# Hybrid decoder trunk on one core: the opening's squares, condition row and first loads moved to other engines and queues

## The chip, the cores and the metric

The kernel runs on 1 core of one Trainium2 chip. The metric is the device time in microseconds. The core has five engines that run side by side and wait for one another by semaphores: TensorE (PE, with its weight loads as PEld), VectorE (DVE), ScalarE (ACT), GpSimd (POOL) and SyncE (SP), which here only issues transfers. Transfers (DMAs) can be issued from SP's queue (hardware queue q1) or from POOL's (software queue q0).

## What is computed

The reference is a two-layer decoder trunk in float32, on x of 512 tokens by 1024 channels. Each layer is a half-step SwiGLU FFN, a token mixer and another half-step FFN; the mixer is a short gated convolution in layer 0 and a sparse attention (NSA) in layer 1. Each of the six sub-layers starts with an RMS norm with shift, scale and gate taken from a condition vector c:

```python
cond = jax.nn.silu(c)
mod = (cond @ ada_w[i] + ada_b[i]).reshape(bsz, 3, 3, D_MODEL)
shift, scl, gate = mod[:, :, 0], mod[:, :, 1], mod[:, :, 2]
h = adaln(x, norm_g[i, 0], shift[:, 0], scl[:, 0])
x = x + HALF * gate[:, 0, None, :] * swiglu(h, ffn_w_in[i, 0], ffn_w_out[i, 0])
```

where `adaln` is `rms_norm(x, g) * (1 + scale) + shift`. For the opening it matters that nothing of the first FFN can be multiplied before the norm of x (the mean square over all 1024 channels of each token) and the first scales and shifts (products of the condition vector with rows of `ada_w`) are there.

## The kernel before, in words

**Layout.** x is held transposed, as eight tiles `x[0]` to `x[7]` of 128 channels by 512 tokens. Products are made in three passes for accuracy: each operand is split into a high part (`hi`, made by ACT, line 164) and a remainder (`lo`, made by DVE, line 165), and `mm3` (lines 167 to 170) multiplies hi by hi, hi by lo and lo by hi. The profile's `whi` and `wlo` are those of a weight tile, `hhi` and `hlo` (lines 285, 286) those of the normed x.

**Loads ahead of the work** (lines 89 to 93). SP's queue issues six x tiles and then `cond`, which is c read 128 times from DRAM so that each partition has the whole row; POOL's queue issues the last two x tiles, the norm gains `ngs` and the biases `adabs`. Then POOL makes the identity `ident`. ACT turns cond into its Silu at line 107.

**Modulation** (`ada_tile`, line 115). One tile is 128 rows of the transposed `ada_w`, 512 KB, loaded on SP's queue into a buffer `adaraw`, of which the pool `ada` has four. DVE multiplies it by cond and sums along the row in one instruction (line 119) to 128 values of `mods`. There are 144 such tiles. `ada_scale` and `ada_shift` (lines 123 to 131) add the biases and gains. `ada_first` (line 141) makes the 16 tiles of the first sub-layer's scale and shift, two for each channel block d, in pairs of blocks from d = 2 on. `ada_jobs` makes the others, spread over the following work.

**The first norm** (`Norm.start`, line 261, under high priority). ACT squares each x tile (line 266), DVE adds the squares into `nacc` (line 268), four products with a column of ones sum `nacc` over the partitions into a PSUM tile `pr` (line 270), DVE takes the mean (`nv`, line 272) and the reciprocal root by Newton steps (`rsqrt`, lines 195 to 204), scales the identity by it (`dg`, line 277), and two products with a matrix of ones spread it over all partitions (line 278). `Norm.whole(d)` (line 281) then makes `xr` (DVE, line 284), `hhi` (ACT) and `hlo` (DVE) of block d.

**The first FFN** (`ffn_first`, line 419). Its opening is a loop over the eight blocks d: modulate block d, load and split one of six head weights while d < 6 (`ffn_in`, which calls `weights`; loads at line 179 on SP's queue), norm block d, and multiply it into all head products whose weights are there. The six products accumulate in six PSUM tiles `hs`. After them come the ordinary tiles (`pair`, products named `gu`), whose weights `weights` loads on SP's queue too. The raw weights have three buffers in the pool `wp`, used by the first three head weights, and two in the pool `ada` for the others.

**What sets the order.** Nothing is ordered by hand on the engines: the framework takes the instructions of each engine by the order of the program and by priority, and may put an instruction that it finds ready ahead of one that it finds waiting. A queue of transfers is issued in order, so a load that waits for a buffer holds back those behind it.

Of the kernel before, what the change touches and what calls it, by code (L numbers as in the profile page):

```python
# [12 lines left out]
F32 = mybir.dt.float32  # L13
F32R = mybir.dt.float32r
I32 = mybir.dt.int32
AF = mybir.ActivationFunctionType
ALU = mybir.AluOpType
# [4 lines left out]
P = 128  # L22
D = 1024
T = 512
HT = T // 2
KD = D // P
# [4 lines left out]
NB = T // P  # L31
# [12 lines left out]
NADA = 24  # L44
# [8 lines left out]
def decoder_kernel(ctx, tc, xT, cT, ng, adaw, adab, ffi, ffo, cwi, cw, cwo,  # L53
                   nwi, nwg, pos, w1, w2, qg, kg, nwo, rb, onehot, rowok, out):
    nc = tc.nc
# [15 lines left out]
    def psum(name, tag="mm"):  # L71
        tag = next(six) if tag == "mm" else {"pr": "o"}.get(tag, tag)
        return ps.tile([P, T], F32, name=name, tag=tag, bufs=2)
# [4 lines left out]
    def tmp(name, n=T, tag="t"):  # L78
        bufs, size = TAGS[tag]
        return tp.tile([P, n], F32, name=name, tag=tag, padded_shape=[P, size], bufs=bufs)  # L80


    ada_es = ctx.enter_context(ExitStack())
    ap = ada_es.enter_context(tc.tile_pool(name="ada", bufs=4))
    cond = ap.tile([P, D], F32, name="cond", bufs=1)
    x = [cst.tile([P, T], F32, name=f"x{d}") for d in range(KD)]
    ngs = cst.tile([P, NSUB * KD], F32, name="ngs")
    adabs = cst.tile([P, NSUB * NMOD], F32, name="adabs")
    for d in range(KD):
        (nc.sync if d < KD - 2 else nc.gpsimd).dma_start(x[d], xT[d])  # L90
    nc.sync.dma_start(cond, bass.AP(tensor=cT.tensor, offset=cT.offset, ap=[[0, P], [1, D]]))
    nc.gpsimd.dma_start(ngs, ng)
    nc.gpsimd.dma_start(adabs, adab)
    one = ap.tile([P, 1], F32, name="one", bufs=1)
# [4 lines left out]
    ones = cst.tile([P, P], F32, name="ones")  # L99
# [4 lines left out]
    rowm = cst.tile([P, 1], F32, name="rowm")  # L104
    mods = cst.tile([P, NSUB * NMOD], F32, name="mods")

    nc.scalar.activation(cond, cond, AF.Silu)

    def mod(s, kind, d):
        c = s * NMOD + kind * KD + d  # L110
# [1 line left out]

    def ada_tile(ap, s, t):
        raw = ap.tile([P, D], F32, name="adaraw")
        nc.sync.dma_start(raw, adaw[s * NADA + t])
        m = mods[:, s * NMOD + t:s * NMOD + t + 1]
        nc.vector.tensor_tensor_reduce(out=raw, in0=raw, in1=cond, scale=1.0, scalar=0.0,  # L119
                                       op0=ALU.mult, op1=ALU.add, accum_out=m)  # L120
# [21 lines left out]
    def ada_first(ap, d):  # L142
        n = 1 if d < 2 else 2
        if d % n == 0:
            for c in range(d, d + n):
                ada_tile(ap, 0, c)
                ada_tile(ap, 0, KD + c)
            ada_scale(0, d, d + n)
            ada_shift(0, d, d + n)

# [18 lines left out]
        nc.tensor.matmul(o, sh, ml, start=False, stop=False)  # L169
        nc.tensor.matmul(o, sl, mh, start=False, stop=last)  # L170

    def weights(src, nk, ncol, own=None, held=3, raws=None, to=None):
        def part(name, dt, bufs, from_):
            return (from_ or wp).tile([P, nk * ncol], dt, name=name, tag=name, padded_shape=[P, KD * P], bufs=bufs)

        hi, lo = to or (part("whi", F32R, held, own), part("wlo", F32R, held, own))
        raws = raws or own
        raw = part("wraw", F32, 3 if raws in (None, wp) else 2, raws)
        nc.sync.dma_start(raw.rearrange("p (a n) -> p a n", a=src.shape[1]), src)
        split(raw, hi, lo)  # L180
        return [t.rearrange("p (k n) -> p k n", n=ncol) for t in (hi, lo)]

# [35 lines left out]
    class Norm:  # L218
# [42 lines left out]
        def start(self):  # L261
            pv = self.all = psum("pr", "pr")
            with tc.high_priority():
                for d in range(KD):
                    dst = self.acc if d == 0 else tmp("sq", tag="sq")
                    nc.scalar.activation(dst, x[d], AF.Square)
                    if d:
                        nc.vector.tensor_tensor(self.acc, self.acc, dst, ALU.add)
                for t in range(NB):
                    nc.tensor.matmul(pv[:, t:t + 1], self.acc[:, t * P:(t + 1) * P], ones[:, 0:1], start=True, stop=True)  # L270
                v = sp.tile([P, NB], F32, name="nv", tag="nv", padded_shape=[P, NB])
                nc.vector.tensor_scalar(v, pv[:, 0:NB], 1.0 / D, EPS, op0=ALU.mult, op1=ALU.add)
                r = rsqrt(v, NB)
                dg = tmp("dg").rearrange("p (a b) -> p a b", a=NB)
                for hf in range(2):
                    for t in range(2 * hf, 2 * hf + 2):
                        nc.vector.tensor_scalar(dg[:, t, :], ident, r[:, t:t + 1], None, op0=ALU.mult)
                    nc.tensor.matmul(self.all[:, hf * HT:(hf + 1) * HT], ones,
                                     dg[:, 2 * hf:2 * hf + 2].rearrange("p a b -> p (a b)"), start=True, stop=True)
# [97 lines left out]
        return fill  # L377


    def ffn_in(f, j, c, own=None):  # L380
        return weights(ffi[f, j, c], KD, P, own)


    def ffn_out(f, d, m, j0, j1, own=None):
# [34 lines left out]
    def ffn_first(s, f, nrm, nxt, extra, ahead, first, soon, own):  # L419
        with ExitStack() as es:  # L420
            hp = pool(es, "hp", 1)
            hid = Hidden(es, 18)
            h = nrm.alloc(hp)
            nj = FIRST
            early = spread(soon, PARTS[0][1] - nj)
            late = spread(extra, NJ - PARTS[0][1] + 2 * KD)

            def fill():
                early() if soon else late()

            js = [(j, c) for j in range(nj) for c in range(2)]
            w, os = [], [psum("hs") for _ in js]
            for d in range(KD):
                first(d)
                if d < len(js):
                    w.append(ffn_in(f, *js[d], own=own if d > 2 else None))
                nrm.whole(d)
                for n in range(len(w)):
                    for k in range(0 if n == d else d, d + 1):
                        project(os[n], w[n], 0, h, [(k, k)], k == 0, k == KD - 1)  # L440
            for j in range(nj):
                hid.activate(os[2 * j], os[2 * j + 1])
            for p, (j0, j1) in enumerate(PARTS):
                for j in range(max(j0, nj), j1):
                    hid.activate(*pair(f, j, h, own))
                    fill()
                n = j1 - j0
                a, ka = (hid.hi[j0:j1], hid.lo[j0:j1]), [(k, k) for k in range(n)]
                last = p == len(PARTS) - 1
                for d in range(KD - 3 if last else KD):  # L450
                    w = ffn_out(f, d, 1, j0, j1, own if d % 2 else None)
                    o = psum("y")
                    project(o, w, 0, a, ka, True, True)
                    if last:
                        residual(s, d, o, nxt)
                    else:
                        fill()
                        nc.vector.scalar_tensor_tensor(x[d], o, mod(s, 2, d), x[d], op0=ALU.mult, op1=ALU.add)
            assert not extra
            return tail(s, nxt, [(d, ffn_out(f, d, 1, j0, j1, own), 0, ka) for d in range(KD - 3, KD)], a, ahead)  # L460
# [839 lines left out]
```

## Time and profile before

| | us |
|---|---|
| median of 3 runs | 2037.07 |
| lowest, highest | 2033.68, 2041.28 |
| the profiled execution | 2035.68 |
| its span, first to last instruction | 2033.9 |

The profile is of one execution. Its page lists the busy time of each engine, the span in 40 slices, the DMA queues, the chain of work that ended last, and groups of instructions by line, engine and tile. The views used below are the table by stretches (busy time of each engine in each), the timeline (start, duration, engine, line, tile written and tiles read), groups of instructions (count, busy us, mean ns and the idle time before them), the chain of work in order of time, and the list of DMA issues (KB of each, median us from issue to landing). `L119` is line 119 of the kernel before. `SPq` and `POOLq` are the queues of those engines.

### The profile page before, as it was taken

How to read it: one execution, taken by the hardware profiler on the slowest of the kernel's cores; microseconds unless marked ns; L12 is line 12 of the kernel's file. 1: busy time of each engine (PE TensorE's matmuls, PEld its weight loads, DVE VectorE, ACT ScalarE, POOL GpSimd, SP SyncE). 2: the span in 40 equal slices, each digit the busy share in tenths (PEclk: the TensorE clock that was granted, in tenths of full speed). 3: DMA queues.
4: the chain of work that ended last, by engine and by line, in shares of the span. 5: the costliest groups of instructions: out<-in, count | busy, mean ns of one | idle time of the engine just before them, and what ended most of it. 6: DMA issues, size and time to landing. Idle time of an engine off the chain costs nothing.

```text
span 2033.9 us, 32445 instructions
## 1 busy us (share of the span) xinstructions
PE 1962.4 (96%) x12644; PEld 1766.0 (87%) x12644; DVE 1494.8 (73%) x2597; ACT 875.3 (43%) x1410; POOL 202.1 (10%) x279
## 2 busy tenths in 40 slices
PE   5999999999998999999999999999999898999999
PEld 3878888888897898999989899999888788898989
DVE  7888888664467586768768676886887886686865
ACT  3322222332244343434534343455777755343532
POOL 0000000100011000000100000002354520000000
PEclk9999999999998999999999999999999999999999
DMA  8889988322237464533646453133111125565621
GB/s 303 301 311 320 333 317 323 141 97 83 83 84 199 123 171 137 153 114 84 184 137 172 137 153 113 45 137 104 53 51 49 58 63 142 145 169 146 167 78 63
DMA packets 113046, 307.39 MB, mean 151 GB/s; under 512 B 13883, under 2 KB 14155, under 8 KB 112892
## 3 DMA queue, kind: packets, MB, share of 16 engines
q1 hardware_dynamic: 97164, 274.81, 39.2%
q0 software_dynamic: 15728, 30.51, 8.6%
q8 instruction: 99, 1.62, 0.3%
q14 instruction: 55, 0.45, 0.1%
HBM read 302.12 MB, written 3.15 MB: 150 GB/s over the span
## 4 chain that ended last, share of the span: by engine, by line
PE 83%; DVE 8%; ACT 4%; DMA 2%; issue 2%; SPq 0%; POOL 0%; ACTq 0%; DVEq 0%; POOLq 0%
PE gu L168 13%; PE gu L169 13%; PE gu L170 13%; PE y L168 7%; PE y L169 7%; PE y L170 7%; PE cv L169 2%; PE cv L168 2%; PE hs L168 2%; PE hs L169 2%; PE cv L170 2%; PE hs L170 2%; DVE wlo L165 1%; PE ty L169 1%; PE ty L168 1%
## 5 line engine op out<-in xcount | busy, mean ns | idle before, releaser
L164 ACT ACTIVATE whi<-wraw 128x1024 fp32r<-128x1024 f32 (+2 forms) x286 | 285.3, 1001 | 552.0 <-PE y L169 262.8
L165 DVE TENSOR_TENSOR wlo<-wraw,whi 128x1024 fp32r<-128x1024 f32 (+2 forms) x286 | 330.0, 1157 | 65.2 <-ACT whi L164 62.1
L168 PE MATMUL gu<-hhi,whi 128*128 128x256 f32 (+1 forms) x856 | 273.8, 320 | 4.3 <-ACT whi L164 4.2
L169 PE MATMUL gu<-hlo,whi 128*128 128x256 f32 (+1 forms) x856 | 273.8, 320 | 0.0
L170 PE MATMUL gu<-hhi,wlo 128*128 128x256 f32 (+1 forms) x856 | 272.0, 318 | 0.2 <-DVE wlo L165 0.2
L168 PE MATMUL y<-ahi,whi 128*128 128x512 f32 x587 | 230.6, 395 | 0.2 <-ACT ahi L164 0.2
L170 PE MATMUL y<-ahi,wlo 128*128 128x512 f32 x587 | 230.7, 396 | 0.0
L169 PE MATMUL y<-alo,whi 128*128 128x512 f32 x587 | 230.4, 395 | 0.0
L119 DVE CUSTOM_DVE_ANT_0 adaraw<-adaraw,cond 128x1024 f32<-128x1024 f32 x144 | 173.4, 1222 | 21.1 <-DMA adaraw<-in_adaw 20.0
L168 PEld LDWEIGHTS gu<-hhi,whi 128*128 128x128 f32 x856 | 161.5, 189 | 19.8 <-ACT whi L164 5.6
L169 PEld LDWEIGHTS gu<-hlo,whi 128*128 128x128 f32 x856 | 161.4, 189 | 13.1
L170 PEld LDWEIGHTS gu<-hhi,wlo 128*128 128x128 f32 x856 | 160.8, 188 | 13.7 <-DVE wlo L165 0.6
L488 POOL DMA_DIRECT2D qa<-in_ffi x57 | 68.6, 1204 | 838.2 <-DVE qal L165 240.1
L168 PE MATMUL gu<-th,qah 128*128 128x256 f32 x456 | 130.1, 285 | 12.3 <-ACT p L515 12.3
L168 PEld LDWEIGHTS y<-ahi,whi 128*128 128x128 f32 x587 | 109.5, 188 | 29.2 <-ACT ahi L164 3.3
L169 PEld LDWEIGHTS y<-alo,whi 128*128 128x128 f32 x587 | 110.2, 188 | 27.9 <-DVE alo L165 1.8
L170 PEld LDWEIGHTS y<-ahi,wlo 128*128 128x128 f32 x587 | 110.2, 188 | 25.6
L557 DVE SCALAR_TENSOR_TENSOR x<-y,mods,x 128x512 f32<-128x512 f32 x72 | 54.0, 750 | 106.2 <-PE y L170 106.2
L168 PE MATMUL gu<-th,qbh 128*128 128x256 f32 x456 | 128.2, 281 | 2.4 <-ACT qbh L164 2.4
L169 PE MATMUL gu<-tl,qah 128*128 128x256 f32 x456 | 129.5, 284 | 0.0
L170 PE MATMUL gu<-th,qbl 128*128 128x256 f32 x456 | 128.4, 282 | 0.7 <-DVE qbl L165 0.7
L170 PE MATMUL gu<-th,qal 128*128 128x256 f32 x456 | 129.0, 283 | 0.0
(295 smaller groups left out, 5146.9 us busy)
## 6 DMA issues: line engine op xcount, KB each, us to landing
adaraw<-in_adaw SPq DMA_DIRECT2D x144, 512.0 KB, 5.6
wraw<-in_ffi SPq DMA_DIRECT2D x119, 512.0 KB, 3.7
qa<-in_ffi SPq DMA_DIRECT2D x114, 256.0 KB, 3.9
qa<-in_ffi POOLq DMA_DIRECT2D x57, 512.0 KB, 5.7
wraw<-in_ffo SPq DMA_DIRECT2D x72, 384.0 KB, 3.8
a<-in_ffi SPq DMA_DIRECT2D x57, 256.0 KB, 3.6
wraw<-in_cwi SPq DMA_DIRECT2D x24, 512.0 KB, 3.3
wraw<-in_nwi SPq DMA_DIRECT2D x20, 512.0 KB, 3.4
```

Of the source, the lines that this page charges most:

```text
L119: nc.vector.tensor_tensor_reduce(out=raw, in0=raw, in1=cond, scale=1.0, scalar=0.0, op0=ALU.mult, op1=ALU.add, accum_out=m)
L164: nc.scalar.activation(hi, src, AF.Copy)
L165: nc.vector.tensor_tensor(lo, src, hi, ALU.subtract)
L168: nc.tensor.matmul(o, sh, mh, start=first, stop=False)
L169: nc.tensor.matmul(o, sh, ml, start=False, stop=False)
L170: nc.tensor.matmul(o, sl, mh, start=False, stop=last)
L488: nc.gpsimd.dma_start(qa, bass.AP(tensor=a21.tensor, offset=a21.offset, ap=[a21.ap[0], [0, 2], a21.ap[1]]), accum_op=ALU.add)
L557: nc.vector.scalar_tensor_tensor(x[d], o, mod(s, 2, d), x[d], op0=ALU.mult, op1=ALU.add)
```

## The change

The change has five parts.

- The eight x tiles are all issued on SP's queue. c is loaded as one row of 4 KB into the first partition of an `adaraw` buffer, first on POOL's queue; the load of c into all partitions goes.
- Two products of a row of ones with that row spread it over the partitions, 512 columns each, into PSUM, and ACT takes the Silu from there.
- The squares are no longer added by DVE. Each of them goes to four products with the column of ones, which accumulate over the eight tiles in `pr`.
- The 16 tiles of `ada_first` and the six head weights are issued on POOL's queue; all other modulation tiles and weights stay on SP's.
- The pool `ada` has five buffers instead of four.

```diff
     ada_es = ctx.enter_context(ExitStack())
-    ap = ada_es.enter_context(tc.tile_pool(name="ada", bufs=4))
+    ap = ada_es.enter_context(tc.tile_pool(name="ada", bufs=5))
     cond = ap.tile([P, D], F32, name="cond", bufs=1)
     x = [cst.tile([P, T], F32, name=f"x{d}") for d in range(KD)]
     ngs = cst.tile([P, NSUB * KD], F32, name="ngs")
     adabs = cst.tile([P, NSUB * NMOD], F32, name="adabs")
+    crow = ap.tile([P, D], F32, name="adaraw")[0:1]
+    nc.gpsimd.dma_start(crow, cT)
     for d in range(KD):
-        (nc.sync if d < KD - 2 else nc.gpsimd).dma_start(x[d], xT[d])
-    nc.sync.dma_start(cond, bass.AP(tensor=cT.tensor, offset=cT.offset, ap=[[0, P], [1, D]]))
+        nc.sync.dma_start(x[d], xT[d])
     nc.gpsimd.dma_start(ngs, ng)
     nc.gpsimd.dma_start(adabs, adab)
     one = ap.tile([P, 1], F32, name="one", bufs=1)
...
     rowm = cst.tile([P, 1], F32, name="rowm")
     mods = cst.tile([P, NSUB * NMOD], F32, name="mods")
-    nc.scalar.activation(cond, cond, AF.Silu)
+
+    for c in range(D // T):
+        o = psum("cb", "nat")
+        nc.tensor.matmul(o, ones[0:1], crow[:, c * T:(c + 1) * T], start=True, stop=True)
+        nc.scalar.activation(cond[:, c * T:(c + 1) * T], o, AF.Silu)
     def mod(s, kind, d):
         c = s * NMOD + kind * KD + d
...
-    def ada_tile(ap, s, t):
+    def ada_tile(ap, s, t, queue=None):
         raw = ap.tile([P, D], F32, name="adaraw")
-        nc.sync.dma_start(raw, adaw[s * NADA + t])
+        (queue or nc.sync).dma_start(raw, adaw[s * NADA + t])
         m = mods[:, s * NMOD + t:s * NMOD + t + 1]
         nc.vector.tensor_tensor_reduce(out=raw, in0=raw, in1=cond, scale=1.0, scalar=0.0,
                                        op0=ALU.mult, op1=ALU.add, accum_out=m)
...
         n = 1 if d < 2 else 2
         if d % n == 0:
             for c in range(d, d + n):
-                ada_tile(ap, 0, c)
-                ada_tile(ap, 0, KD + c)
+                ada_tile(ap, 0, c, nc.gpsimd)
+                ada_tile(ap, 0, KD + c, nc.gpsimd)
             ada_scale(0, d, d + n)
             ada_shift(0, d, d + n)
...
         nc.tensor.matmul(o, sh, ml, start=False, stop=False)
         nc.tensor.matmul(o, sl, mh, start=False, stop=last)
-    def weights(src, nk, ncol, own=None, held=3, raws=None, to=None):
+    def weights(src, nk, ncol, own=None, held=3, raws=None, to=None, queue=None):
         def part(name, dt, bufs, from_):
             return (from_ or wp).tile([P, nk * ncol], dt, name=name, tag=name, padded_shape=[P, KD * P], bufs=bufs)
         hi, lo = to or (part("whi", F32R, held, own), part("wlo", F32R, held, own))
         raws = raws or own
         raw = part("wraw", F32, 3 if raws in (None, wp) else 2, raws)
-        nc.sync.dma_start(raw.rearrange("p (a n) -> p a n", a=src.shape[1]), src)
+        (queue or nc.sync).dma_start(raw.rearrange("p (a n) -> p a n", a=src.shape[1]), src)
         split(raw, hi, lo)
         return [t.rearrange("p (k n) -> p k n", n=ncol) for t in (hi, lo)]
...
             pv = self.all = psum("pr", "pr")
             with tc.high_priority():
                 for d in range(KD):
-                    dst = self.acc if d == 0 else tmp("sq", tag="sq")
-                    nc.scalar.activation(dst, x[d], AF.Square)
-                    if d:
-                        nc.vector.tensor_tensor(self.acc, self.acc, dst, ALU.add)
-                for t in range(NB):
-                    nc.tensor.matmul(pv[:, t:t + 1], self.acc[:, t * P:(t + 1) * P], ones[:, 0:1], start=True, stop=True)
+                    sq = tmp("sq", tag="sq")
+                    nc.scalar.activation(sq, x[d], AF.Square)
+                    for t in range(NB):
+                        nc.tensor.matmul(pv[:, t:t + 1], sq[:, t * P:(t + 1) * P], ones[:, 0:1],
+                                         start=(d == t == 0), stop=(d == KD - 1 and t == NB - 1))
                 v = sp.tile([P, NB], F32, name="nv", tag="nv", padded_shape=[P, NB])
                 nc.vector.tensor_scalar(v, pv[:, 0:NB], 1.0 / D, EPS, op0=ALU.mult, op1=ALU.add)
                 r = rsqrt(v, NB)
...
         return fill
-    def ffn_in(f, j, c, own=None):
-        return weights(ffi[f, j, c], KD, P, own)
+    def ffn_in(f, j, c, own=None, queue=None):
+        return weights(ffi[f, j, c], KD, P, own, queue=queue)
     def ffn_out(f, d, m, j0, j1, own=None):
...
             for d in range(KD):
                 first(d)
                 if d < len(js):
-                    w.append(ffn_in(f, *js[d], own=own if d > 2 else None))
+                    w.append(ffn_in(f, *js[d], own=own if d > 2 else None, queue=nc.gpsimd))
                 nrm.whole(d)
                 for n in range(len(w)):
                     for k in range(0 if n == d else d, d + 1):
```

## The prediction

> **What bounds the kernel now.** I read the head of the page first.
>
> ```profile
> span 2033.9 us, 32445 instructions
> PE 1962.4 (96%) x12644; PEld 1766.0 (87%) x12644; DVE 1494.8 (73%) x2597; ACT 875.3 (43%) x1410; POOL 202.1 (10%) x279
> ```
>
> TensorE (PE) is idle for 2033.9 - 1962.4 = 71.5 us in all, and an edit to the opening can win only what of that lies in the opening. The table by stretches says how much (columns: stretch, length, busy us of PE, weight loads, DVE, ACT, POOL, clock, DMA share, GB/s).
>
> ```profile
> 0.00:16.30 16.30, 1.87 (x8) 1.78 (x8) 5.33 (x10) 7.46 (x11) 3.08 (x10) 1.00 0.89 317
> 16.30:25.40 9.10, 2.08 (x4) 1.18 (x4) 8.78 (x28) 1.76 (x3) 0.00 (x0) 1.00 0.56 203
> 25.40:44.70 19.30, 15.79 (x50) 10.70 (x50) 19.30 (x38) 7.39 (x9) 0.00 (x0) 1.00 0.93 327
> 44.70:66.60 21.90, 21.85 (x94) 17.75 (x95) 18.18 (x33) 6.29 (x10) 0.00 (x0) 1.00 0.83 307
> 66.60:200.00 133.40, 133.40 (x570) 106.61 (x569) 110.22 (x166) 39.93 (x50) 0.00 (x0) 1.00 0.88 314
> ```
>
> From 44.7 us on PE has no gap until past 200 us. Whatever moves the 44.7 us point moves the end by as much, and whatever only adds transfers or DVE work after it is hidden. Before it the stretches have different limits. Between 16.3 and 44.7 us DVE is full (19.30 of 19.30). Between 16.3 and 25.4 us the DMA engines are only 0.56 busy: the modulation rows wait for buffers that DVE has not freed. The chain of work that ended last names what stands ahead of 16.3 us, and the timeline what ends it.
>
> ```profile
> 2.59 7.93 DMA x<-in_xT
> 10.60 0.64 ACT sq L266
> 13.66 0.70 DVE nacc L268
> 14.40 1.88 PE pr L270 x8
> ...
> 43.56 1.15 DVE wlo L165
> 44.75 0.50 PE hs L170
> ```
>
> ```profile
> 16.31 0.16 DVE L272 TENSOR_SCALAR nv<-pr 128x4 f32<-128x4 f32 x1 [1.96 <-PE pr L270]
> 16.63 1.23 DVE L119 CUSTOM_DVE_ANT_0 adaraw<-adaraw,cond 128x1024 f32<-128x1024 f32 x1
> 13.33 1.04 ACT L107 ACTIVATE cond<-cond 128x1024 f32<-128x1024 f32 x1
> ```
>
> The last x tile lands at 2.59 + 7.93 = 10.5 us, the squares are added up by DVE until 14.4, TensorE sums them over the partitions by 16.3, and only then does DVE touch its first modulation row: the Silu of cond ran at 13.33, behind all eight squares. So DVE starts at 16.3 a queue of work that it finishes without a break.
>
> **The change, part by part.** The opening's DVE work, between 16.3 and 57.3 us, by groups:
>
> ```profile
> L119 DVE CUSTOM_DVE_ANT_0 adaraw<-adaraw,cond 128x1024 f32<-128x1024 f32 x17 | 20.4, 1224 | 0.0
> L165 DVE TENSOR_TENSOR wlo<-wraw,whi 128x1024 fp32r<-128x1024 f32 x6 | 7.3, 1222 | 0.0
> L284 DVE SCALAR_TENSOR_TENSOR xr<-x,mods,pr 128x512 f32<-128x512 f32 x8 | 5.9, 746 | 0.0
> L268 DVE TENSOR_TENSOR nacc<-nacc,sq 128x512 f32<-128x512 f32 x7 | 4.8, 692 | 8.2 <-ACT sq L266 7.7
> ```
>
> 1. *Squares by TensorE.* Seven DVE additions go (4.8 us), all before 16.3 us, where DVE is otherwise idle; this frees DVE for rows but shortens nothing alone. In their place TensorE does 8 x 4 products of one column, two passes each: 64 passes instead of 8. Their price stands in two rows, an early one and a late one.
>
> ```profile
> 14.40 1.87 PE L270 MATMUL pr<-ones,nacc 128*128 128x1 f32 x8 [14.40 <-DVE nacc L268]
> 397.91 0.58 PE L250 MATMUL pr<-ones,nacc 128*128 128x1 f32 x4
> 21.39 2.08 PE L278 MATMUL pr<-dg,ones 128*128 128x256 f32 x4 [5.12 <-DVE dg L277]
> 403.43 0.70 PE L258 MATMUL pr<-dg,ones 128*128 128x256 f32 x2
> ```
>
> 1.87/8 = 0.234 us a pass on a TensorE that has just begun, 0.58/4 = 0.145 on one long at work: 64 passes are 15.0 or 9.3 us. The table's clock column reads 1.00 in the opening too, so the difference shows in the durations only.
>
> 2. *cond by matmuls.* Two one-row products of 512 columns, two passes each: four passes of twice 2.08/4 = 0.52, so 4.2 us, or twice 0.70/2 = 0.35, so 2.8 us. TensorE has nothing else before 14.4 us, but they queue with the square sums. One Silu of 1.04 us becomes two of about 0.6 us, on an ACT busy 7.46 of 16.3 us. The broadcast load of cond (0.52 MB, at 327 GB/s 1.6 us of the DMA engines) goes. The row of c now leads POOL's queue:
>
> ```profile
> 1.28 1.31 POOL L90 DMA_DIRECT2D x<-in_xT  x2 [0.83 <-POOLq L1289]
> 2.58 0.55 POOL L92 DMA_DIRECT2D ngs<-in_ng  x1
> L488 POOL DMA_DIRECT2D qa<-in_ffi x57 | 68.6, 1204 | 838.2 <-DVE qal L165 240.1
> x<-in_xT POOLq DMA_DIRECT2D x2, 256.0 KB, 6.9
> 17.89 8.27 SPq L117 DMA_DIRECT2D adaraw<-in_adaw  x4
> ```
>
> It lands between about 3.5 us (nothing ahead of it) and 1.28 + 6.9 = 8.2 us; with matmuls and Silu cond is ready between 7 and 13 us. I take 9. Before, it was 14.4.
>
> 3. *Sixteen rows and six head weights through POOL.* The 22 issues cost POOL between 0.55 us (ngs) and 1.20 us (the L488 row) each: 12 to 26 us over some 45, on an engine with 0.00 busy from 16.3 to 66.6 us, so nothing. The row loads wait for a free buffer, and head weights 2 to 5 stand behind them in the queue; on SP it was the same (four issues took 8.27 us from 17.89 on). The identity needed for the norm's spread is made on POOL in program order ahead of the first row, so it does not get stuck. SP gets two more x issues (about 0.43 us each). Rows now overtake x at the DMA engines: last x at 10.5 us if it loses nothing, 16 if the rows take half from the start; I take 12.
>
> 4. *Fifth row buffer.* One is c's until the second cond matmul, then five rows can be under way instead of four. Where DVE is the limit (0.0 idle in the groups above) it is worth nothing; it matters only between cond and the norm.
>
> **The sum.** When is the norm's sum ready (16.3 before)? TensorE starts at about 4.1 us, when the second square ran before. All slow passes: 4.1 + 15.0 + 4.2 = 23.3. By the x tiles alone: 10.5 + 0.6 + 8 passes x 0.234 + 0.3 = 13.3. The head products turn from 0.42 to 0.23 us apart some 8 us after the first one, so I take 8 us slow (cond and 16 sums), then 48 x 0.145 = 7.0: 4.1 + 8 + 7 = 19.1 and, as the first may speed up sooner, **18 us**: 1.7 later.
>
> ```profile
> 25.47 0.79 PE L168 MATMUL hs<-hhi,whi 128*128 128x512 f32 x1 [2.01 <-ACT hhi L285]
> 27.44 0.63 PE L170 MATMUL hs<-hhi,wlo 128*128 128x512 f32 x1
> 27.86 0.63 PE L169 MATMUL hs<-hlo,whi 128*128 128x512 f32 x1
> 35.53 0.40 PE L168 MATMUL hs<-hhi,whi 128*128 128x512 f32 x1
> 35.76 0.40 PE L169 MATMUL hs<-hlo,whi 128*128 128x512 f32 x1
> ```
>
> What can DVE do by then? 18 us at 317 GB/s move 5.7 MB, less 2.2 of x and small tables 3.5 MB, which is six transfers of 0.52: rows 1 and 2, weight 0, rows 3 and 4, weight 1. Each then costs DVE 1.14 us ahead of the norm instead of behind it (a 1.15 us step stands in the chain above). Before, two rows ran inside the norm's chain of small steps: 16.31 to 20.85 with them, and 13 steps 0.2 us apart (2.5 us) without, so these two give 2.0 us.
>
> ```profile
> 19.79 0.16 DVE L203 TENSOR_TENSOR rs_b<-rs_a,nv 128x4 f32<-128x4 f32 x1
> 19.99 0.16 DVE L204 SCALAR_TENSOR_TENSOR rs_r<-rs_b,rs_r 128x4 f32<-128x4 f32 x1
> 20.85 0.87 DVE L277 TENSOR_SCALAR dg<-ident,rs_r 128x128 f32<-128x128 f32 x4
> ```
>
> Gain at the 44.7 us point: 2.0 + 4 x 1.14 - 1.7 = **4.9 us**. The bounds of the unknowns nearly cancel, since a later norm lets more rows pass: ready at 13.3, three transfers are in, 2.0 + 1.14 + 3.0 = 6.1; ready at 23.3, nine (seven rows, two weights), 2.0 + 7 x 1.14 - 7.0 = 3.0. Late next is DVE still, and then TensorE itself: first head product at about 20.6, and 144 of them at 0.233 us (33.6) end no sooner than 54, against 66.6 before.
>
> The profiled execution took 2035.68 us (span 2033.9, and 1.78 around it); 2035.68 - 4.9 = 2030.8. It lay 1.39 us under the median of 2037.07, so I forecast 2037.07 - 4.9 = **2032.2 us**.
>
> **The rivals.**
>
> *A. The transfers become the limit.* Up to 46 us:
>
> ```profile
> DMA packets 4249, 13.73 MB, mean 299 GB/s; under 512 B 506, under 2 KB 522, under 8 KB 4248
> ```
>
> The opening needs 2.2 (x, tables) + 16 x 0.52 + 6 x 0.52 = 13.7 MB without cond. If 299 GB/s is all that the engines give, that is again 46 us, and the gain is cond's 1.6 us: **2035.5**. For it: share 0.93 from 25.4 to 44.7. Against: share 0.56 from 16.3 to 25.4, 4 us of slack. [...]
>
> *B. SP runs ahead (slower).* SP has nothing left in front of the next weights and the gate rows, which before were issued only behind row 16:
>
> ```profile
> 43.90 1.16 SPq L179 DMA_DIRECT2D wraw<-in_ffi  x2
> ```
>
> They can now take row and weight buffers and DMA time out of turn. Each costs 0.52/327 = 1.6 us; the slack is 4.0 us plus cond's 1.6, so it decides from the fourth such transfer on. With eight (five weight and three row buffers, 8 x 1.6 = 12.8 us) the opening's last data come 12.8 - 5.6 = 7.2 us later than before: **2044.3**. Against it: those buffers come free only after the first splits, and SP's order kept to the program's before.
>
> *C. TensorE's small products are the new chain.* All passes stay at 0.234 us, the norm is ready at 23.3, gain 3.0: **2034.1**. [...]
>
> **How the numbers follow.** Forecast (gain 3 to 6.1 us, so 2031 to 2034) 0.55; A 0.18; C 0.14; B 0.13. A measurement of this kernel tells about 0.5% (10.2 us) from no change, and no worked case but a worse B (ten transfers or more ahead: 16 - 5.6 = 10.4 us) passes that. Half of B, 0.06, is slower; 0.05, taken from the forecast, is left for a gain of over 10 us, for which norm and rows would both have to come far sooner; 0.89 is within. The three executions before spread over 2033.68 to 2041.28, so I widen 2031 to 2035.5 by 4 us downwards, and upwards to half of B: 2027 to 2041.
>
> **What would show it.** Right: the first modulation row on DVE at 9 to 12 us instead of 16.63, four rows or more ahead of L272, that instruction at 13 to 23 us, the stretch in which DMA stood at 0.56 filled, and the first gu product some 5 us before 66.6. A shows as DVE waiting for adaraw in the opening; B as SP loads of wraw for later tiles, or of gate rows, before 25 us, with weights 3 to 5 late; C as TensorE without gaps from 4 us to L272. Wrong altogether I would be if gaps opened past 66.6 us, where the order of instructions may change and I count nothing.

## The result and the profile after

| | before | after |
|---|---|---|
| median of 12 runs each, us | 2033.38 | 2046.1 |
| ratio after to before, 95% interval | | 1.0055 [1.0035, 1.0075] |
| the profiled execution, us | 2035.68 | 2042.2 |
| its span, us | 2033.9 | 2040.4 |

The change makes the kernel slower by 0.55%. The forecast was a gain, and the time lies above its range. The same table by stretches, with the same cuts, shows where (columns as before: stretch, length, busy us of PE, weight loads, DVE, ACT, POOL, clock, DMA share, GB/s).

```profile
0.00:16.30 16.30, 12.12 (x42) 9.08 (x42) 2.04 (x7) 6.45 (x10) 6.67 (x17) 1.00 0.88 322
16.30:25.40 9.10, 6.08 (x29) 6.00 (x30) 2.74 (x17) 1.26 (x2) 0.00 (x0) 1.00 0.44 143
25.40:44.70 19.30, 9.67 (x19) 5.42 (x20) 16.62 (x32) 5.95 (x8) 4.71 (x9) 1.00 0.65 240
44.70:66.60 21.90, 21.90 (x89) 17.48 (x88) 20.81 (x38) 4.54 (x6) 2.63 (x5) 1.00 0.96 363
66.60:200.00 133.40, 133.40 (x564) 106.39 (x563) 113.78 (x175) 41.69 (x52) 0.00 (x0) 0.99 0.88 316
```

Read the third row against its counterpart: TensorE was busy for 15.79 us of that stretch and is now busy for 9.67, and 4 of its 19 passes are the norm's spread. DVE, full before from 16.3 us on, is busy for 2.74 of 9.10 us in the second row; and the DMA share there, which was to be filled from 0.56 up, falls to 0.44. From the fourth row on TensorE has no gap, as before. The opening's loss is thus carried to the end: the first `gu` product, at 66.62 us before, comes at 76.53.

```profile
66.62 0.39 PE L168 MATMUL gu<-hhi,whi 128*128 128x512 f32 x1
```

```profile
76.53 0.39 PE L173 MATMUL gu<-hhi,whi 128*128 128x512 f32 x1
```

That is 9.9 us later, and the ratio makes 0.0055 x 2033.38 = 11.2 us (0.0035 to 0.0075: 7.1 to 15.3). The rest of the run, span less first `gu`, took 1967.3 us before and 1963.9 after; over the profiles below it lies anywhere between 1959 and 1975. So the start of the first `gu` is the closer measure of the opening, and the table below uses it beside the ratio; but it is read from one profiled execution of each kernel, so differences of a microsecond mean little.

The chain of work that ended last, in order of time, names what stands in the opening now (start, us, what).

```profile
3.50 0.64 ACT sq L271
4.18 1.87 PE pr L273 x8
6.05 2.00 PE cb L111 x2
8.05 1.80 PE pr L273 x8
9.85 2.00 PE cb L111 x2
11.84 10.34 PE pr L273 x48
...
25.19 2.09 PE pr L282 x4
27.31 0.75 DVE xr L288
28.05 1.14 DVE adaraw L124
```

Two things are to be seen. First, from 4.18 to 22.2 us the chain is nothing but TensorE: 64 one-column passes and four passes that spread c. Forty-eight of them take 10.34 us, 0.215 each, near the early price of 0.234; they never speed up. Second, the step behind the norm's first `xr` is a modulation row at 28.05 us. It is row 2, which ran at 18.26 us before, inside the norm's chain:

```profile
18.26 1.22 DVE L119 CUSTOM_DVE_ANT_0 adaraw<-adaraw,cond 128x1024 f32<-128x1024 f32 x1
```

DVE's timeline (start, us, engine, line, what, and in brackets the idle time before it with its releaser) shows what DVE of the changed kernel did until then.

```profile
12.51 1.22 DVE L124 CUSTOM_DVE_ANT_0 adaraw<-adaraw,cond 128x1024 f32<-128x1024 f32 x1 [11.21 <-ACT cond L112]
...
22.21 0.16 DVE L276 TENSOR_SCALAR nv<-pr 128x4 f32<-128x4 f32 x1 [8.08 <-PE pr L273]
...
27.31 0.75 DVE L288 SCALAR_TENSOR_TENSOR xr<-x,mods,pr 128x512 f32<-128x512 f32 x1 [1.59 <-PE pr L282]
27.97 1.22 DVE L124 CUSTOM_DVE_ANT_0 adaraw<-adaraw,cond 128x1024 f32<-128x1024 f32 x1
```

One row, then 8.08 us of waiting for the norm's sum, then the norm, and only behind `xr` the second row. It was not the data: the transfers up to 22.2 us (busy tenths of the DMA engines in 40 slices, the sum of all, then POOL's queue) carry 4.30 MB on POOL's queue, which is six rows and two weights of 0.52 MB, the row of c and the two small tables, and they had all landed by about 21 us.

```profile
DMA  0006699899999999999999999999999999983000
DMA packets 3068, 6.55 MB, mean 295 GB/s; under 512 B 955, under 2 KB 971, under 8 KB 3068
q0 software_dynamic: 1248, 4.30, 51.7%
```

So the data lay there and DVE waited beside them. And because DVE did not free the buffers, POOL could issue nothing more: its timeline has a hole of 14.93 us, and head weights 2 and 3 come behind it (SP issued its pair for them at 26 us before, POOL now at 34.31).

```profile
14.04 0.53 POOL L122 DMA_DIRECT2D adaraw<-in_adaw  x1 [1.36 <-DVE mods L130]
29.49 0.53 POOL L122 DMA_DIRECT2D adaraw<-in_adaw  x1 [14.93 <-DVE mods L136]
...
34.31 1.04 POOL L184 DMA_DIRECT2D wraw<-in_ffi  x2
```

In the stretch from 22.2 to 31.1 us the DMA engines are 0.03 busy. By 44.7 us TensorE has begun 15 `hs` products, against 50 before.

### The profile page after: what moved, and what is told of

It reads as the page before. It is cut to its first block, busy times and chain, and to the rows that moved or that the text cites. A ratio compares the mean times of both kernels' runs of the same rounds, so it can differ in the third digit from the quotient of the medians.

```text
span 2040.4 us, 32524 instructions
## 1 busy us (share of the span) xinstructions
PE 1972.4 (97%) x12704; PEld 1772.9 (87%) x12704; DVE 1488.8 (73%) x2590; ACT 874.2 (43%) x1411; POOL 213.6 (10%) x300
## 4 chain that ended last, share of the span: by engine, by line
PE 84%; DVE 8%; ACT 3%; issue 2%; DMA 2%; SPq 0%; POOL 0%; DVEq 0%; ACTq 0%; POOLq 0%
PE gu L173 13%; PE gu L175 13%; PE gu L174 13%; PE y L173 7%; PE y L174 7%; PE y L175 7%; PE hs L174 2%; PE hs L173 2%; PE hs L175 2%; PE cv L174 2%; PE cv L173 2%; PE cv L175 2%; DMA qa<-in_ffi 2%; PE ty L174 1%; PE ty L173 1%
```

## The experiments

My theory after reading the traces had two parts. *T*: the one-column passes on TensorE make the norm late. *O*: the change altered the order of DVE's instructions, which I took to be laid out when the program is built: rows that have landed stand behind the norm's waiting instruction. The rivals were *N*, that the late norm alone does everything, so that all is well once DVE adds the squares again; and *G*, that transfers issued by GpSimd are the cost in themselves. In the expectations, which were written before each run, "theory N" is this *N*, and "theory Q" is *O* as far as the loads' queue sets the order.

All runs in one table, by the profile of each: first modulation row on DVE, start of `nv` (the norm's sum is there), first `hs`, number of `hs` products begun before 44.7 us, first `gu`; and the ratio to the kernel before on the same chip.

| kernel | first row | nv | first hs | hs by 44.7 | first gu | ratio [95%] |
|---|---|---|---|---|---|---|
| before | 16.63 | 16.31 | 25.47 | 50 | 66.62 | 1 |
| after | 12.51 | 22.21 | 31.14 | 15 | 76.53 | 1.0055 [1.0035, 1.0075] |
| squares back on DVE | 12.55 | 16.57 | 28.45 | 22 | 74.10 | 1.0031 [1.0014, 1.0047] |
| squares alone | 21.15 | 19.62 | 28.80 | 32 | 70.63 | 1.0034 [1.0018, 1.0050] |
| loads back on SP | 23.19 | 22.25 | 31.43 | 28 | 73.23 | 1.0044 [1.0024, 1.0064] |
| rows first | 12.25 | 25.49 | 36.16 | 26 | 72.16 | 1.0034 [1.0015, 1.0053] |
| queue alone | 18.12 | 18.05 | 25.85 | 32 | 71.78 | 1.0016 [1.0000, 1.0032] |
| condition row alone | 12.32 | 14.36 | 22.44 | 59 | 64.49 | 0.9971 [0.9954, 0.9988] |
| rows first, tables held | 12.62 | 19.63 | 30.30 | 52 | 66.06 | 1.0000 [0.9984, 1.0016] |
| squares back, tables held | 12.57 | 16.57 | 25.51 | 34 | 71.38 | 1.0006 [0.9992, 1.0019] |
| the same, norm behind row 2 | 12.52 | 16.53 | 26.72 | 61 | 63.96 | 0.9972 [0.9956, 0.9987] |
| condition row, four buffers | 11.48 | 13.52 | 21.60 | 64 | 63.30 | 0.9988 [0.9972, 1.0005] |

**Squares back on DVE.** After, with the sum of squares as it was.

```diff
-                    sq = tmp("sq", tag="sq")
-                    nc.scalar.activation(sq, x[d], AF.Square)
-                    for t in range(NB):
-                        nc.tensor.matmul(pv[:, t:t + 1], sq[:, t * P:(t + 1) * P], ones[:, 0:1],
-                                         start=(d == t == 0), stop=(d == KD - 1 and t == NB - 1))
+                    dst = self.acc if d == 0 else tmp("sq", tag="sq")
+                    nc.scalar.activation(dst, x[d], AF.Square)
+                    if d:
+                        nc.vector.tensor_tensor(self.acc, self.acc, dst, ALU.add)
```

> The changed kernel with the squares added by DVE again; all other parts of the change stay. Theory N (the 64 slow one-column passes on TensorE make the norm's sum late: 22.2 us against 16.3): the sum is back at 15 to 16 us and nearly all of the loss goes, ratio to the kernel before 0.998 to 1.001. Theory Q (the loads on GpSimd's queue: DVE's order has the second modulation row behind the norm instead of inside it): the first head product stays at 26 us or later and the ratio stays at 1.003 to 1.005.

The norm's sum is back at 16.57 us, 5.6 us sooner than after, but the first `gu` comes only 2.4 us sooner. The first head product at 28.45 us and the ratio of 1.0031 are what was set down for the order, not for *N*. *N* falls: with the norm as early as before, three quarters of the loss at the first `gu` stay (74.10 - 66.62 = 7.5 of 9.9 us). DVE's waits in the opening (in total, times, longest) show something new.

```profile
DVE rbn L662 <- DMA rbs<-in_rb: 2.8, 1, 2.8
DVE xr L289 <- PE pr L283: 1.8, 1, 1.8
DVE qgs L1210 <- DMA qgs<-in_qg: 1.5, 1, 1.5
```

`qgs` and `rbs` are tables of 0.5 and 2 KB for the attention layer; the first instruction that uses `qgs` in earnest ran at 1376.9 us in the kernel before, and its load was issued at 77.2. With the rows gone from SP's queue the tables are loaded right behind x (`qgs` at 5.28 us in the kernel after), and their DVE instructions have moved from 83.7 us and later into the norm's chain, where DVE waits for them. Of the two waits only the 2.8 us for `rbs` lengthens the chain: that for `qgs` ends at 16.14 us, 0.4 us before TensorE has the sum ready. Row 2 and those behind it still stand behind `xr`.

**Squares alone.** Before, with only the sum of squares changed to the products of the change (the diff above, the other way round).

> The kernel before with the squares summed by TensorE, nothing else of the change. Cond's Silu stays late. Theory N: the norm's sum comes at 18 to 19 us (64 passes of 0.217 us from 4.2 us on, no cond products between), 2 to 3 us late, ratio 1.001 to 1.003. Theory Q: 1.000, since the rows stay where they were in DVE's order.

```profile
4.07 3.57 PE L268 MATMUL pr<-ones,sq 128*128 128x1 f32 x16 [4.07 <-ACT sq L266]
9.19 10.40 PE L268 MATMUL pr<-ones,sq 128*128 128x1 f32 x48 [1.54 <-ACT sq L266]
```

Again 3.57/16 = 0.223 and 10.40/48 = 0.217 us a pass. The sum is ready at 19.6 instead of 16.3 us, and the first `gu` comes 4.0 us later (1.0034). This is a little more than was set down for the late sum (18 to 19 us, ratio 1.001 to 1.003). *T* stands by itself: this part of the change costs about 4 us, and nothing in the opening pays it back. In the full change the four passes of c stand among the sums, and these end at 22.2: 2.6 us more.

**Loads back on SP.** After, with the rows and head weights of the first FFN issued on SP's queue.

```diff
-                ada_tile(ap, 0, c, nc.gpsimd)
-                ada_tile(ap, 0, KD + c, nc.gpsimd)
+                ada_tile(ap, 0, c)
+                ada_tile(ap, 0, KD + c)
...
-                    w.append(ffn_in(f, *js[d], own=own if d > 2 else None, queue=nc.gpsimd))
+                    w.append(ffn_in(f, *js[d], own=own if d > 2 else None))
```

> The changed kernel with the 16 first rows and the six head weights on SP's queue again. Theory N: the norm's sum stays at 22 us and the ratio at 1.003 to 1.006. Theory Q: rows stand inside and right behind the norm's chain again, as before, and the ratio falls to 1.000 to 1.002.

Now no row at all runs ahead of the norm (first row 23.19), yet the first `gu` is 3.3 us sooner than after: two rows go inside the norm's chain and two more ahead of the first `hlo`, just as in the kernel before. The place of the rows in DVE's order changes with the queue that loads them, though nothing else in the program does. The ratio does not show this gain: 1.0044 lies where *N* had it (1.003 to 1.006), not where the order had it (1.000 to 1.002), and its interval overlaps that of the whole change. With the sums on TensorE 6.6 of the 9.9 us at the first `gu` stay whatever the queue.

**Queue alone.** Before, with only those loads moved to POOL's queue (the diff above, the other way round).

> The kernel before with the 16 first rows and six head weights on GpSimd's queue, nothing else. In it the scheduler's order on DVE puts two instructions that wait for small tables (qgs, rbn) in the norm's chain, and xr ahead of rows 3 and on. Theory Q (the queue changes the planned order, so rows keep their buffers until the norm is done and the loads behind them stand still): first gu product 4 to 7 us later than the 66.6 of before, DMA share under 0.5 around the norm, ratio 1.002 to 1.004. Theory N (only the late norm costs): the norm's sum stays near 16.3 us, first gu within 1 us of 66.6, ratio 1.000.

```profile
17.98 0.15 DVE L1205 TENSOR_SCALAR qgs<-qgs 128x1 f32<-128x1 f32 x1 [2.29 <-DMA qgs<-in_qg]
18.05 0.15 DVE L272 TENSOR_SCALAR nv<-pr 128x4 f32<-128x4 f32 x1
18.12 1.22 DVE L119 CUSTOM_DVE_ANT_0 adaraw<-adaraw,cond 128x1024 f32<-128x1024 f32 x1
```

This is a kernel with the old squares and the old condition row, and it shows the same thing: a wait for `qgs` directly in front of `nv`, row 2 at 22.36 us instead of 18.26, and the first `gu` 5.2 us late, in the range set down (the ratio, 1.0016, lies a little under its range and agrees less clearly: 3.3 us, 0 to 6.5). Of the 2.29 us for `qgs` only some 0.4 are a loss, since TensorE ends the sum at 17.60. That sum is itself 1.3 us later than before (16.28): with the rows and head weights on POOL's queue, the only change of this run, the last square starts at 14.12 instead of 12.79.

**Rows first.** After, with the norm's end (from `nv` on) written behind the first two blocks' modulation and head weights, so that DVE has four rows ahead of it.

```diff
+AHEAD = 2
...
+        def spread(self):
+            pv = self.all
+            with tc.high_priority():
...
+            for d in [*range(AHEAD), None, *range(KD)]:
+                if d is None:
+                    with tc.issue_after(newest[0]):
+                        nrm.spread()
```

> The changed kernel with the norm's end (from the mean on) ordered behind the fourth row on DVE, by an order of issue without a wait. The norm's sum stays at 22 us, but DVE should do four rows and one weight remainder before it. If the sum of the prediction was wrong only in that the rows did not stand ahead of the norm, the ratio is 0.998 to 1.001. If the lateness of the norm alone is enough (theory N, with TensorE's products then short of time), it stays at 1.002 or more.

The first `gu` improves by 4.4 us, to 72.16, though the norm itself gets 3.3 us later: buffers come free early and the transfers go on (394 GB/s from 25.5 to 36 us). The ratio stays at 1.0034, which was set down as the sign that the late norm is enough. But here the two tables' waits (2.04 and 4.45 us) stand ahead of rows 2 to 4; how much of the rest is theirs this run doesn't separate.

**Rows first, tables held.** That order, with the squares on DVE, and with the tables' instructions put behind the newest row in DVE's order.

```diff
+        with tc.issue_after(newest[0]):
+            small_now()
```

> The changed kernel with the squares on DVE, the norm's end ordered behind row 4, and the small tables ordered behind the rows traced before them, all by order of issue without waits. The order then is what the prediction took for granted: rows 1 to 4 and weight 0 ahead of the norm's end. If the prediction's sum held but for order and the slow sums, first gu comes at 61 to 64 us (2.0 + 4 x 1.14 earlier than before, less what the norm waits for row 4), ratio 0.997 to 0.999. If the loads come too late to be used ahead of the norm (x and rows share the engines), the norm's end waits for row 4 until about 20 us and first gu is 66 to 70.

DVE is busy for 17.73 of the 18.50 us from 12.6 to 31.1 us, the DMA share is 0.96 up to 31.1 us, and the result is that of before, 1.0000. But much stands ahead of the norm: the sum was there at about 16.6 us and `nv` came at 19.63, behind four rows and a weight, and four rows more stand ahead of the first `xr`. That this is too many is argued from these times; the run with two rows ahead, below, has its first `gu` 2.1 us sooner, and the intervals of the two ratios overlap.

**Squares back, tables held; and the same with the norm's end behind row 2.** These two differ in one thing. In the second, the norm's end is written behind the first block's two rows and head weight (`AHEAD = 1` in the diff above). Both load rows and head weights through POOL.

> The changed kernel with the squares on DVE and the small tables' instructions ordered behind the rows traced before them; rows and head weights stay on GpSimd's queue. In the run with the squares alone taken back, DVE waited 1.5 and 2.8 us for two small tables inside the norm's chain. If those waits are the queue's loss, the first gu product falls from 74.1 to 69 to 71 us and the ratio to about 1.001. If the loss is that row 2 stands behind xr, so that no row buffer comes free until the norm is done, the chain gets shorter but the loads stay as late behind it: first gu 71 to 73, ratio 1.002 to 1.003.

> The same with the norm's end ordered behind row 2 on DVE (issue order only): two row buffers come free before the norm, and rows 3 and 4 fall into its chain. The loads stay on GpSimd's queue. If the order on DVE is what the queue costs, first gu is 64 to 67 us and the ratio 0.997 to 1.000, as with the rows on SP's queue. If transfers issued by GpSimd are themselves slower or later, it stays at 69 us or more and the ratio at 1.001 or more.

Holding the tables takes the norm's chain back to its old pace (first `hs` 25.51, as before), and 2.7 us come back at the first `gu`, as many as the wait for `rbs` was long; 4.8 stay. That is the case set down for row 2 behind `xr`, though the ratio came out better than its 1.002 to 1.003. DVE's timeline of the first of the two, from the norm to the second row:

```profile
16.57 0.16 DVE L278 TENSOR_SCALAR nv<-pr 128x4 f32<-128x4 f32 x1 [1.70 <-PE pr L276]
...
21.67 0.75 DVE L290 SCALAR_TENSOR_TENSOR xr<-x,mods,pr 128x512 f32<-128x512 f32 x1 [1.78 <-PE pr L284]
22.34 1.22 DVE L124 CUSTOM_DVE_ANT_0 adaraw<-adaraw,cond 128x1024 f32<-128x1024 f32 x1
```

And of the second:

```profile
14.75 1.22 DVE L125 CUSTOM_DVE_ANT_0 adaraw<-adaraw,cond 128x1024 f32<-128x1024 f32 x1
...
16.53 0.16 DVE L283 TENSOR_SCALAR nv<-pr 128x4 f32<-128x4 f32 x1 [0.55 <-PE pr L277]
18.19 1.23 DVE L172 TENSOR_TENSOR wlo<-wraw,whi 128x1024 fp32r<-128x1024 f32 x1
...
19.41 1.22 DVE L125 CUSTOM_DVE_ANT_0 adaraw<-adaraw,cond 128x1024 f32<-128x1024 f32 x1
...
20.62 1.22 DVE L125 CUSTOM_DVE_ANT_0 adaraw<-adaraw,cond 128x1024 f32<-128x1024 f32 x1
```

Row 2 fits into the wait for the sum (14.75; `nv` is not later for it), and rows 3 and 4 and a weight go between the norm's small steps. The same two stretches, 16.5 to 25.5 us, of the first and then of the second kernel (columns as in the table above):

```profile
16.50:25.50 9.00, 2.11 (x5) 1.17 (x4) 5.64 (x22) 1.71 (x3) 0.53 (x1) 1.00 0.52 158
```

```profile
16.50:25.50 9.00, 2.07 (x4) 1.17 (x4) 8.73 (x29) 1.06 (x1) 2.40 (x5) 1.00 1.02 363
```

DVE from 5.64 to 8.73 us, transfers from 158 to 363 GB/s, the first `gu` from 71.38 to 63.96, and the ratio from 1.0006 to 0.9972, with intervals apart. The queue is POOL's in both, so *G* falls as the cause of the loss: with a better order, as was set down for it, the same loads belong to a kernel that beats both the one before and the one after. One cost of the queue itself does show, in the kernels with the squares on DVE: with the loads on SP, behind x, the last square starts at 11.06 us and `nv` at 14.36 (the first kernel of the next paragraph), with the loads on POOL at 13.22 to 13.26 and 16.53 to 16.57. x itself lands later there: with the loads on SP none of the last five squares waits, with the loads on POOL (norm behind row 2) the last three wait for x, 0.38, 1.15 and 0.85 us. The norm's sum is 2.2 us later for it.

**Condition row alone; and with four buffers.** The parts of the change that are left: c as one row spread by TensorE, x all on SP, and the fifth buffer; squares on DVE and rows on SP as before. The second kernel has `bufs=4`.

> Of the change, the condition row by matmuls, x on one queue and the fifth buffer; squares on DVE and rows and head weights on SP. Theory Q and theory N both say that neither of the two losses is left: norm's sum at 16 to 17 us, first gu at 65 to 67 us, ratio 0.998 to 1.001. If an early cond is worth what the prediction held (rows ahead of the norm), first gu falls to 62 to 64; the scheduler's order, with one row ahead of the norm, speaks for 65.5.

> The kernel with the condition row by matmuls and x on one queue, all else as before, and four row buffers instead of five. If the fifth buffer is worth nothing, as the prediction had it, first gu is within 0.5 us of 64.5 and the ratio within 0.996 to 0.999. If the gain of that version comes from the fifth buffer, first gu goes back to 66 to 67 and the ratio to 1.000.

The first row on DVE comes at 12.32 instead of 16.63 us, DVE does it and the next one around `nv`, and the first `gu` comes 2.1 us sooner; 0.9971. That lies between the cases set down (62 to 64 and 65 to 67 us), with a better ratio than either named. The norm's sum is earlier too (`nv` 14.36 instead of 16.31), with all of x on SP's queue and the broadcast load gone; how much of the gain is the early row and how much the early sum, no run separates. With four buffers the first `gu` is another 1.2 us sooner, outside the 0.5 us set down, and the ratio is 0.9988 [0.9972, 1.0005]. The intervals of the two overlap, and 0.8 us of the 1.2 are there at `nv` already: the third square starts at 6.21 instead of 7.07 us, before either kernel has issued its third row. So I read no worth of the fifth buffer from them. One part of the change is good alone, and what it wins was lost in the company of the others.

**Wide products among the sums** (one time of 2058.75 us, no interval). After, with eight products of 512 columns ahead of the sums and two more behind each square; nothing reads what they compute.

```diff
+            wide = tp.tile([P, T], F32R, name="wide", tag="t", bufs=4)
+            warm = psum("warm", "s")
...
+                nc.vector.tensor_copy(wide, ones[:, 0:1].to_broadcast([P, T]))
+                for _ in range(8):
+                    nc.tensor.matmul(warm, wide[:, 0:P], wide, start=True, stop=True)
...
+                    for _ in range(2):
+                        nc.tensor.matmul(warm, wide[:, 0:P], wide, start=True, stop=True)
```

> The changed kernel with products added that nothing reads: eight of 512 columns (one pass each) at the start and two ahead of each square's sums. A look at the passes only. If TensorE speeds up by wide products in a row and one-column passes do not count, the one-column passes fall from 0.217 us apart to 0.11 to 0.15 from about 6 us on, and the norm's sum comes at 17 to 20 us in spite of the added work (24 passes of 0.43 or 0.23 us). If it cannot speed up so early, or one-column passes are never faster here, they stay 0.217 apart and the sum comes at 28 us or later.

```profile
1.64 3.78 PE L273 MATMUL warm<-wide 128*128 128x512 f32 x8 [1.64 <-DVE wide L271]
...
6.07 1.26 PE L280 MATMUL pr<-ones,sq 128*128 128x1 f32 x8
7.18 0.71 PE L278 MATMUL warm<-wide 128*128 128x512 f32 x2
7.74 0.95 PE L280 MATMUL pr<-ones,sq 128*128 128x1 f32 x8
...
15.18 1.70 PE L280 MATMUL pr<-ones,sq 128*128 128x1 f32 x8
```

Behind the eight wide products the one-column passes do go fast: 0.95/8 = 0.119 us each by the last row of that kind, 0.158 by the first. By 15 us they are back at 1.70/8 = 0.213, though TensorE has had no pause and about two wide products for every eight narrow passes. The clock column of this run says what happened in between (columns as in the first table):

```profile
5.00:9.00 4.00, 4.00 (x23) 3.37 (x22) 0.00 (x0) 0.86 (x2) 1.77 (x4) 1.00 1.04 378
12.00:15.00 3.00, 3.00 (x10) 2.03 (x9) 1.35 (x3) 1.19 (x2) 0.53 (x1) 0.50 1.05 396
```

The granted clock is 1.00 from 5 to 9 us and 0.50 from 12 to 15; over the whole run it is 0.975, against 0.988 before. Why it fell the run doesn't show. The passes at 0.50 take 0.213 us, about as long as those of the changed kernel, whose column reads 1.00. As a remedy it fails: `nv` at 27.16 us (17 to 20, or 28 and more, had been set down), the first `gu` at 81.98, with the stretch of the low clock ahead of it.

## Why the prediction was wrong, step by step

**What bounds the kernel**: right. The loss at the first `gu` (9.9 us) is that of the run (11.2, 7.1 to 15.3), and past it nothing opened: the rest of the run, 1963.9 us, is no longer than the 1967.3 of before.

**Squares by TensorE** is the term that was mis-sized: the two prices (0.234 or 0.145 us a pass) bracket what came, and I chose between them wrongly. I put the speed-up after 8 us, from head products; the passes stay at 0.234 to 0.217 over 18 us and the sum is ready at 22.2 instead of 18, 5.9 us later than before instead of 1.7. The case of slow passes only, 23.3, was near. Rival C had this mechanism at about its size: 18 us of this work without a gap did not bring the faster pace.

**cond by matmuls**: ready at 12.5 us (11.88 + 0.60), not 9; within my 7 to 13. ACT's second half of the Silu waits for the second pair of c's products, and these stand among the sums (9.85 in the chain). I had said that they queue there and had put no price on it.

**Sixteen rows and six head weights through POOL**: the issues themselves cost POOL 0.53 to 0.58 us each and hold nothing up, as said. But I wrote "on SP it was the same" of the order in the queue, and looked at queues only. The loads' queue entered into the order in which DVE's instructions were laid out: alone it costs 5.2 us at the first `gu`. I looked for SP's freedom in rival B as loads ahead of turn; the price came by another way, through row 2, which moved behind `xr`, and through two tables whose DVE instructions moved into the norm. That the rows overtake x I had foreseen and put at 1.5 us for the last tile (12 for 10.5), but the sum then left it out; with the squares on DVE it measured 2.2 us at `nv`, and in the changed kernel the slow sums hide it, since from 9.93 us on the squares wait for TensorE and not for x.

**Fifth row buffer**: no worth is seen, as said, though it was tried only with the loads on SP's queue.

**The sum** is the step that failed. "Each then costs DVE 1.14 us ahead of the norm instead of behind it", and "a later norm lets more rows pass". Of the six transfers that I counted by 18 us, and of eight that were in by 22.2, DVE took one. I treated DVE as if it took whatever had landed. It took nothing for the 8.08 us in which `nv` waited, with rows landed behind it. What I say ahead of the prediction, that the framework may put a ready instruction ahead of one that waits, can be meant only of the order as it is laid out; while the kernel ran, nothing passed the waiting `nv`. So a later norm did the opposite: it held all that stood behind it. In place of a gain of 4.9 us came 9.9 us of loss at the first `gu`. The one-sided bounds (gain 6.1 to 3.0) followed from the failed sentence, and so no case of mine but B ended slower. Had I set C's 23.3 beside a DVE that doesn't pass, its price would have been 23.3 - 16.3 = 7 us and more, close to what came.

The parts do not add up. Measured singly at the first `gu` they make +4.0 us (squares), +5.2 (queue) and -2.1 (condition row, with x on one queue and the fifth buffer), together 7.1 of 9.9. Put one upon the other, they make the whole: squares +4.0 (70.63), condition row +2.6 (73.23), queue +3.3 (76.53); or, in another order, condition row -2.1 (64.49), queue +9.6 (74.10), squares +2.4 (76.53). So the condition row, a gain alone, is a loss beside the squares, among which its passes stand on TensorE (the sums end 2.6 us later, 22.21 against 19.62), and the price of the queue depends on what stands beside it. That the late sum and DVE's order both take part is shown; no single share of either is.

**The rivals.** A: no; the DMA engines stood at 0.03 for 9 us. C: its mechanism came, a TensorE without a gap from 4.18 us to `nv`, but not its gain of 3.0. B: SP does run ahead (four `wraw` from 32.38 us on, then rows of the gate), but so it does in the best kernel of the POOL queue, from 19.44 us on, with the first `gu` at 63.96; so the loss doesn't need it.

What stays open is why the layout chose that order; the runs show that it changes with the queue and with the place of the norm's end in the program, not by what rule. And for the small differences the first `gu` and the ratio agree only within some 4 us: for the condition row alone 2.1 us sooner against 5.9 (2.4 to 9.4) by the ratio, and for the squares back with the tables held 4.8 us later against 1.2 (-1.6 to 3.9).

## What to carry to other kernels

On DVE nothing passed the instruction that waited (`nv`, 8.08 us, with rows landed): data that came early were of use only where the instruction that uses them stood ahead of the one that waited. So for each wait that a change makes longer, read from the timeline what is behind it on that engine and which buffers it keeps full. Moving loads from one queue to another moved instructions here on an engine that has no part in it (DVE's row 2 from 18.26 to 22.36 us, the first `gu` 5.2 us later); look at its order first, and set the order by hand where it matters (the norm's end behind row 2 instead of ahead of it was worth 7.4 us at the first `gu` here). Price small products in an opening at the slow pace measured there (0.217 to 0.234 us a one-column pass here), and count what they push back on TensorE itself.

## What the hardware showed that I had not expected

- One-column passes did not speed TensorE up here: 0.234 us each in the first eight and 0.217 in the last 48, over 18 us without a gap (the four passes of c among them), though the clock column reads 1.00 throughout. Behind eight products of 512 columns (3.78 us) such passes took 0.158 and then 0.119 us, and 0.213 again at 15 us, where the column of that run reads 0.50 (12 to 15 us). So these passes took about as long under a column of 1.00 in the opening as under one of 0.50 later: here the durations, not the column, told the pace. Why the passes were fast behind the wide products, and why the column then fell to 0.50, is not shown; it is one execution of each.
- A table of half a KB took about 10 us to land when it was issued among the large loads (`qgs`: issued at 5.28 us, median 10.2 us to landing), twice the median of an x tile of 256 KB (5.0 us) in the same list of DMA issues. Issued at 77.25 us in the kernel before, the same table took 4.3 us.

```profile
x<-in_xT SPq DMA_DIRECT2D x8, 256.0 KB, 5.0
qgs<-in_qg SPq DMA_DIRECT2D x1, 0.5 KB, 10.2
```
